# Hybrid encoder layer on one core: the values of the dilated heads are fetched one step earlier, into six buffers instead of four

## The chip, the cores and the metric

The kernel runs on one core of a Trainium2 chip. The core has five engines with a program of their own each: TensorE (PE; its weight loads are shown apart, as PEld), VectorE (DVE), ScalarE (ACT), GpSimd (POOL) and SyncE (SP), which here only issues DMA transfers. Each engine works through its instructions in order and waits on semaphores. The metric is the device time of one execution in microseconds (us), less is better; several runs are summed up by their median. "Granted clock" is the share of its full clock that TensorE was allowed.

## The reference

One encoder layer is applied to a prompt (256 tokens) and to a sample (1024 tokens), model width 1024, all in float32:

```python
h = _rmsnorm(x, g_mix)
z = h @ w_in                       # queries, keys, values of both branches, and the gates
o_a = banded attention, 8 heads, window 128, with a sink
o_b = _dilated_mixture(qb, kb, vb, rel_bias[:, A_HEADS:])
merged = gates[0] * (o_a @ w_branch_a) + gates[1] * (o_b @ w_branch_b)
x = x + merged @ w_out
h = _rmsnorm(x, g_mlp)
x = x + square(relu(h @ w_up)) @ w_down      # then a last _rmsnorm
```

The part that matters is `_dilated_mixture`: three groups of four heads, with (window, dilation) of (128, 1), (512, 4) and (2048, 16). In each group the tokens are sorted by their residue modulo the dilation, every query looks at a band of keys of its own residue, a bias by distance is added, and softmax and the product with the values follow. The three groups' outputs are then mixed by their log-sum-exp.

## The kernel before, in words

The two inputs are treated as 1280 tokens, ten tiles of 128. Products of the layer are split into a high and a low half and done in three matmuls. The work goes in stages: norm and value columns of `w_in`; the other columns of `w_in`, two column blocks at a time ("pairs", function `pair`, line 954), by a seven-product scheme whose matmuls are recorded by one helper (L351, names x, y, z, mm); then the banded attention woven into the last gate columns (L192); the merge and `w_out`; the up and down projections (L351 again). Queries, keys, values and gates pass through DRAM: `scr_qb`, `scr_kb` (queries and keys of the dilated heads, by group), `scr_v` (values), `scr_g` (gates).

The dilated heads are computed by `attention_b`, a generator that is stepped while the last five pairs of columns run. `tick` calls it: at every second call, once all earlier pairs are done, one step of `attention_b` is put between two halves of a product of the pair. The order of every engine's instructions is thus written out by hand; no scheduler moves them.

`attention_b` works on 60 tiles (two pairs of heads, three groups, ten tiles each), two tiles a step. A step of number j (0, 2, 4, ...) issues, in this order:

- `load_v`: the values of two tiles, two or four transfers, from `scr_v` into a buffer named v (L510, queue of SP). A transfer is 128 x 128 float32, 64 KB.
- `values_of`: the product of probabilities and values of tiles j-4 and j-3 on PE (L566, into bank pv), which reads v; then `store_values` copies it out (ACT for one tile, DVE for the other, L271 and L273) and GpSimd's queue writes it to DRAM (L575).
- `transposes` of the probabilities of tiles j-2 and j-1 (PE, L553), copied to SBUF by ACT and DVE.
- `scores` of tiles j and j+1 on PE (L522), then bias and row maximum on DVE (L533, L535).
- `load`: queries and keys of tiles j+4 and j+5 into a buffer named qk (L498, L499, queue of SP; four buffers, so that it has to wait for the scores just issued).
- `exponentials` of tiles j and j+1 on ACT (L543).

SP's queue takes all of these loads in the order of the program, and between them the gate stores (L864, which wait for the tile z that ACT or DVE write) and, at the start of each pair, the two 512 KB blocks of raw weights for the next pair (L381). SP waits at an instruction whose operands are not ready, and everything behind it waits too. Each transfer on this queue also waits for the one issued eight before it: their completions share eight semaphores in turn.

Before the change step j fetches the values of tiles j-2 and j-1, and they are used one step later. Four v buffers hold the tiles of two steps.

After the last pair comes the banded attention's start: its first weights are fetched at L222, its queries, keys and values at L429 to L450, and a part of h returns from DRAM at L622; its first scores are L1071.

Of the kernel before, what the change touches and what calls it, by code (L numbers as in the profile page):

```python
# [15 lines left out]
P = 128  # L16
# [81 lines left out]
def encoder_kernel(  # L98
# [37 lines left out]
    def bank(tag, name=None):  # L136
        return psum.tile([P, 512], F32, name=name or tag, tag=tag, bufs={"mm": 3, "sc": 2, "pt": 2, "pv": 1}[tag])
# [333 lines left out]
    def values_rows(g, i, kt):  # L471

        c = (0, 256, 512 + P)[g] + P * i
        if kt >= 8:
            rows = scr_v[NS:, c : c + P]
            return rows[P * (kt - 8) : P * (kt - 7), :] if g == 0 else rows[kt - 8 :: 2, :]
        rows = scr_v[:NS, c : c + P]
        if g == 0:
            return rows[P * kt : P * kt + P, :]
        return rows[kt // 2 :: 4, :][P * (kt % 2) : P * (kt % 2) + P, :] if g == 1 else rows[kt::8, :]  # L480

    def attention_b(make):
# [4 lines left out]
        n = len(order)  # L487
        held, live, bias = {}, {}, {}
        turned_s = slot("pt", (P, 2, 4, P))

        def load(j):

            if j >= n:
                return
            g, i, t, (pieces, W, _) = order[j]
            qk = held[j] = [make("qk", (P, 3 * P), n=4), None]
            for a, (p0, m, qa, ka) in enumerate(pieces):
                nc.sync.dma_start(qk[0][:, p0 : p0 + m], scr_qb[g][i][:, qa : qa + m])  # L498
                nc.sync.dma_start(qk[0][:, P + P * a : P + P * a + W], scr_kb[g][i][:, ka : ka + W])  # L499
            if t == 0:  # L500
                bias[g, i] = load_bias_b(g, i, make)

        def load_v(j):
            if not 0 <= j < n:
                return
            g, i, t, (pieces, W, _) = order[j]
            v = held[j][1] = make("v", (P, 2, P), n=4)
            for a, (_, _, _, ka) in enumerate(pieces):
                for k in range(W // P):
                    nc.sync.dma_start(v[:, a + k, :], values_rows(g, i, ka // P + k))  # L510

        def scores(j):

            banks = [bank("sc") for _ in range(2)]
            at = lambda k, h: banks[h][:, 2 * P * (k - j) : 2 * P * (k - j) + order[k][3][1]]
            for k in (j, j + 1):
                g, i, t, (pieces, W, c0) = order[k]
                qk = held[k][0]
                for h in range(2):
                    rows = HALVES[h]  # L520
                    for a, (p0, nq, _, _) in enumerate(pieces):
                        nc.tensor.matmul(at(k, h)[p0 : p0 + nq, :], qk[rows, p0 : p0 + nq],  # L522
                                         qk[rows, P + P * a : P + P * a + W], start=True, stop=True,
                                         skip_group_check=True)
            for k in (j, j + 1):
                g, i, t, (pieces, W, c0) = order[k]
                whole, *flat = bias[g, i]
                b = whole[:, :, c0 : c0 + W] if c0 is not None else flat[pieces[0][2] >= NS]
                s = make("s", (P, 2, 2 * P), n=2)
                m = small.tile([P, 2], F32, name="m", tag="m")  # L530
                o = make("o", (P, ROW), n=8)
                for h in range(2):
                    nc.vector.tensor_tensor_reduce(s[:, h, :W], at(k, h), b[:, h, :], 1.0, -3.0e38,  # L533
                                                   op0=ALU.add, op1=ALU.max, accum_out=m[:, h : h + 1])
                nc.vector.tensor_scalar(o[:, 2 * HD : 2 * HD + 2], m, -1.0, None, op0=ALU.mult)  # L535
                live[k] = s, o

        def exponentials(j):
            W = order[j][3][1]
            s, o = live[j]  # L540
            nm, l = o[:, 2 * HD : 2 * HD + 2], o[:, 2 * HD + 2 :]
            for h in range(2):
                nc.scalar.activation(s[:, h, :W], s[:, h, :W], AF.Exp, bias=nm[:, h : h + 1],  # L543
                                     accum_out=l[:, h : h + 1])

        def transposes(j, eng):
            W = order[j][3][1]
            s, o = live[j]
            pt = turned_s[:, j % 2]
            ps = bank("pt")  # L550
            jobs = [(k, h) for k in range(W // P) for h in range(2)]
            for a, (k, h) in enumerate(jobs):
                nc.tensor.transpose(ps[:, P * a : P * a + P], s[:, h, P * k : P * k + P], ident)  # L553
            a = len(jobs)
            moved(eng, pt[:, :a, :], ps[:, : P * a].rearrange("p (i q) -> p i q", q=P))
            live[j] = pt, o

        def values_of(j, whole):

            _, _, _, (pieces, W, _) = order[j]  # L560
            pt, v = live[j][0], held.pop(j)[1]
            pv = whole[:, P * (j % 2) : P * (j % 2) + P]
            for h in range(2):
                for a, (p0, nq, _, _) in enumerate(pieces):
                    for k in range(W // P):
                        nc.tensor.matmul(pv[p0 : p0 + nq, HD * h : HD * h + HD], pt[:, 2 * k + h, p0 : p0 + nq],  # L566
                                         v[:, a + k, HALVES[h]], start=k == 0, stop=k == W // P - 1,
                                         skip_group_check=True)

        def store_values(j, eng, whole):  # L570
            g, i, _, (pieces, _, _) = order[j]
            o = live.pop(j)[1]
            moved(eng, o[:, : 2 * HD], whole[:, P * (j % 2) : P * (j % 2) + P])
            for p0, nq, qa, _ in pieces:
                nc.gpsimd.dma_start(scr_b[g][qa : qa + nq, i, :], o[p0 : p0 + nq, :])  # L575
# [6 lines left out]
        yield  # L582
        yield
        for j in range(0, n + 4, 2):
            load_v(j - 2)
            load_v(j - 1)
            if j > 2:
                pv = bank("pv")
                values_of(j - 4, pv)
                values_of(j - 3, pv)  # L590
                store_values(j - 4, nc.scalar, pv)
                store_values(j - 3, nc.vector, pv)
            if 0 < j <= n:
                transposes(j - 2, nc.scalar)
                transposes(j - 1, nc.vector)
            if j < n:
                scores(j)
            load(j + 4)
            load(j + 5)
            if j < n:  # L600
                exponentials(j)
                exponentials(j + 1)
            yield
# [245 lines left out]
    if True:  # L849
# [179 lines left out]
        for first, last, name in ((0, MIXED, "pairs"), (MIXED, len(PAIRS), "mixed")):  # L1029
            with tc.tile_pool(name=name, bufs=1) as now[0]:  # L1030
                if first:
                    att_b = attention_b(stage)
                for j in range(first, last):
                    if j == len(PAIRS) - 1:
                        hooks = entering()
                    else:
                        hooks = line(j, stage) if j < len(LINES) else iter(())
                    b, p = pair(b, p, PAIRS[j], PAIRS[j + 1] if j + 1 < len(PAIRS) else None, hooks, tick, first)
                run(att_b)
                flush(True)  # L1040
# [160 lines left out]
    if True:  # L1201
# [62 lines left out]
        n = len(order)  # L1264
# [96 lines left out]
        for i, (x, b, c) in enumerate(jobs):  # L1361
            t0, n = BLOCKS[b]
# [179 lines left out]
    class Down:  # L1542
# [4 lines left out]
        def make(self, name, shape=(P, 2, 512), dt=F32):  # L1547
            return self.late.tile(list(shape), dt, name=name, tag="l4", bufs=8)
# [334 lines left out]
```

## Time and profile before

| | |
|---|---|
| median of 3 runs | 1751.15 us (1749.18 to 1754.4) |
| profiled execution, its own time | 1753.6 us |
| its span, first to last instruction | 1751.8 us |
| PE busy | 1713.2 us, 98% of the span |
| DVE, ACT, POOL busy | 976.2, 727.1, 518.8 us |
| mean granted clock of TensorE | 0.996 |
| the stage of the dilated heads | from about 358 to 549 us of the span |

Lines of the profile name the source line, the engine and the tiles written and read: "L566 PE pv<-v,pt" is the values product. "SPq" is the queue of SP, where an instruction issues a transfer; "landing" is the moment when a transfer's completion is seen. A wait is given as who waited, and for whom. In the chain of waits each row is a start, a duration and what the time went to.

### The profile page before, as it was taken

The numbers are of one execution on the slowest core, as the hardware profiler recorded it, in microseconds if no ns is written. First come the engines' busy times: TensorE is split into PE (matmuls) and PEld (weight loads), VectorE is DVE, ScalarE is ACT, GpSimd is POOL, SyncE is SP. The second block draws the span as 40 slices with busy tenths as digits, with TensorE's granted clock in tenths as the row PEclk, the third lists the DMA queues.
The fourth block names the chain that finished last, engine by engine and source line by source line (L and its number), as shares of the span: only waits on it lengthen the run. The fifth ranks groups of instructions, "written<-read, shape, count | busy, mean of one in ns | idle before, by whom it ended". The sixth has DMA issues, their size and how long they took to land.

```text
span 1751.8 us, 25171 instructions
## 1 busy us (share of the span) xinstructions
PE 1713.2 (98%) x9248; PEld 1459.5 (83%) x9248; DVE 976.2 (56%) x1708; ACT 727.1 (42%) x1528; POOL 518.8 (30%) x452
## 2 busy tenths in 40 slices
PE   7999999999999999999999999999999999999998
PEld 6898888878788899978888788888888788888886
DVE  6732323455453466676648645454546876657575
ACT  6232223355553455664336433334334333333344
POOL 0212222212221344300010156454655441305050
PEclk9999999999999999999999999999999999999999
DMA  6414344566555662475212243344336854633333
GB/s 235 143 43 153 98 134 120 144 182 169 162 155 143 211 184 81 124 261 214 94 49 97 84 146 120 118 153 153 117 115 240 299 170 145 221 112 117 114 114 120
DMA packets 214779, 256.35 MB, mean 146 GB/s; under 512 B 24887, under 2 KB 144523, under 8 KB 214528
## 3 DMA queue, kind: packets, MB, share of 16 engines
q1 hardware_dynamic: 201424, 228.26, 40.4%
q0 software_dynamic: 12144, 24.38, 4.6%
q10 hardware_dynamic: 1088, 2.10, 0.3%
q8 instruction: 73, 1.20, 0.3%
q14 instruction: 50, 0.41, 0.1%
HBM read 169.10 MB, written 90.73 MB: 148 GB/s over the span
## 4 chain that ended last, share of the span: by engine, by line
PE 85%; DVE 5%; DMA 4%; ACT 3%; issue 2%; SPq 1%; POOL 1%; DVEq 0%; ACTq 0%; POOLq 0%
PE dn L351 20%; PE x L351 17%; PE mm L192 13%; PE z L351 8%; PE v L739 5%; PE pv L351 5%; PE y L351 4%; PE mm L351 4%; PE pv L1108 2%; PE pv L566 2%; DMA v<-scr_v 1%; PE sc L522 1%; PE pt L1095 1%; PE pt L553 1%; PE tr L342 1%
## 5 line engine op out<-in xcount | busy, mean ns | idle before, releaser
L351 PE MATMUL dn<-dhi,ulo 128*128 128x512 f32 x448 | 174.6, 390 | 2.6 <-DVE ulo L186 2.6
L351 PE MATMUL dn<-dhi,uhi 128*128 128x512 f32 x448 | 174.3, 389 | 0.0
L351 PE MATMUL dn<-dlo,uhi 128*128 128x512 f32 x448 | 174.3, 389 | 0.0
L351 PE MATMUL x<-chi,wlo 128*128 128x512 f32 x424 | 167.8, 396 | 2.0 <-DVE u L1756 1.4
L351 PE MATMUL x<-clo,whi 128*128 128x512 f32 x424 | 165.9, 391 | 0.1
L351 PE MATMUL x<-chi,whi 128*128 128x512 f32 x424 | 165.1, 389 | 0.0
L318 DVE TENSOR_TENSOR wlo<-ta,whi 128x1024 fp32r<-128x1024 f32 x30 | 55.8, 1858 | 181.7 <-ACT whi L316 181.7
L318 DVE TENSOR_TENSOR wlo<-raw,whi 128x1024 fp32r<-128x1024 f32 x60 | 89.1, 1484 | 101.9 <-ACT whi L316 101.9
L393 POOL TENSOR_TENSOR tb<-raw 128x512 f32<-128x512 f32 x25 | 33.3, 1333 | 361.5 <-PE mm L192 137.7
L351 PEld LDWEIGHTS dn<-dhi,ulo 128*128 128x128 f32 x448 | 84.1, 188 | 21.0 <-DVE ulo L186 3.6
L186 DVE TENSOR_TENSOR ulo<-uraw,uhi 128x1024 fp32r<-128x1024 f32 x56 | 95.0, 1717 | 11.7 <-ACT uhi L185 11.7
L351 PEld LDWEIGHTS dn<-dlo,uhi 128*128 128x128 f32 x448 | 84.1, 188 | 17.4
L351 PEld LDWEIGHTS dn<-dhi,uhi 128*128 128x128 f32 x448 | 84.1, 188 | 17.4
L351 PEld LDWEIGHTS x<-chi,wlo 128*128 128x128 f32 x424 | 79.9, 188 | 20.7 <-issue 3.4
L351 PEld LDWEIGHTS x<-chi,whi 128*128 128x128 f32 x424 | 79.7, 188 | 17.1
L351 PEld LDWEIGHTS x<-clo,whi 128*128 128x128 f32 x424 | 79.9, 189 | 14.8 <-DVE clo L318 0.4
L1581 POOL TENSOR_TENSOR t<-raw,t 128x1024 f32<-128x1024 f32 x16 | 46.8, 2940 | 141.8 <-DMA raw<-in_w_down_dram 141.8
L1732 DVE TENSOR_TENSOR v<-v,dn 128x512 f32<-128x512 f32 x90 | 59.5, 682 | 43.1 <-PE dn L351 38.5
L1828 POOL TENSOR_TENSOR u<-u,u 128x640 f32<-128x640 f32 x16 | 25.6, 1597 | 164.4 <-ACT u L1753 164.4
L351 PE MATMUL pv<-phi,wlo 128*128 128x256 f32 x256 | 72.5, 283 | 1.7 <-ACT u L1752 1.7
L543 ACT ACTIVATE s<-s,o 128x128 f32<-128x128 f32 (+1 forms) x120 | 51.9, 434 | 52.3 <-DVE o L535 48.3
L351 PE MATMUL dn<-dhi,up 128*128 128x512 f32 x224 | 73.5, 389 | 0.0
(337 smaller groups left out, 4784.8 us busy)
## 6 DMA issues: line engine op xcount, KB each, us to landing
scr_u<-u SPq DMA_DIRECT2D x112, 320.0 KB, 2.6
uraw<-scr_u SPq DMA_DIRECT2D x56, 512.0 KB, 4.2
raw<-in_w_in_dram SPq DMA_DIRECT2D x33, 512.0 KB, 5.5
raw<-in_w_up_dram SPq DMA_DIRECT2D x32, 512.0 KB, 5.5
raw<-in_w_down_dram SPq DMA_DIRECT2D x28, 512.0 KB, 6.2
sg<-scr_g SPq DMA_DIRECT2D x32, 256.0 KB, 5.4
uraw<-scr_u SPq DMA_DIRECT2D x28, 256.0 KB, 4.2
v<-scr_v SPq DMA_DIRECT2D x96, 64.0 KB, 2.3
```

The source lines that it names most:

```text
L186: nc.vector.tensor_tensor(lo, src, hi.bitcast(F32), op=ALU.subtract)
L192: nc.tensor.matmul(ps, a, b, start=i == 0, stop=i == len(seq) - 1)
L318: nc.vector.tensor_tensor(lo, src, hi.bitcast(F32), op=ALU.subtract)
L351: nc.tensor.matmul(ps, a, b, start=first and i == 0, stop=last and i == len(seq) - 1, skip_group_check=True)
L393: (nc.vector if vector else nc.gpsimd).tensor_tensor(o, x, y, op=ALU.subtract)
L543: nc.scalar.activation(s[:, h, :W], s[:, h, :W], AF.Exp, bias=nm[:, h : h + 1], accum_out=l[:, h : h + 1])
L566: nc.tensor.matmul(pv[p0 : p0 + nq, HD * h : HD * h + HD], pt[:, 2 * k + h, p0 : p0 + nq], v[:, a + k, HALVES[h]], start=k == 0, stop=k == ...
L739: nc.tensor.matmul(ps[:, :n], a, b, start=k == 0 and j == 0, stop=k == KC - 1 and j == 2)
L1108: nc.tensor.matmul(pv[:, HD * h : HD * h + HD], pt[:, 2 * b + h, :], src, start=b == 0, stop=b == W // P - 1)
L1581: nc.gpsimd.tensor_tensor(o, a, b, op=ALU.subtract)
L1732: nc.vector.tensor_tensor(v, v, ps, op=ALU.add)
L1828: nc.gpsimd.tensor_tensor(u[S1], u21, u22, op=ALU.add)
```

## The change

Step j now fetches the values of tiles j and j+1, whose scores are computed in the same step, instead of those of tiles j-2 and j-1. They are used two steps later instead of one. The tiles of three steps are then held at once, so v has six buffers instead of four; a buffer is 1 KB in each partition. The first step, which fetched no values, now fetches those of the first two tiles; the fetches end one step earlier than before. The program issues the same 96 transfers. On PE, DVE, ACT and GpSimd the order of the work stays as it was; on SP the fetches stand in the same places with other tiles.

```diff
@@ def load_v(j):
             g, i, t, (pieces, W, _) = order[j]
-            v = held[j][1] = make("v", (P, 2, P), n=4)
+            v = held[j][1] = make("v", (P, 2, P), n=6)
             for a, (_, _, _, ka) in enumerate(pieces):
                 for k in range(W // P):
                     nc.sync.dma_start(v[:, a + k, :], values_rows(g, i, ka // P + k))
@@ the loop of attention_b
         for j in range(0, n + 4, 2):
-            load_v(j - 2)
-            load_v(j - 1)
+            load_v(j)
+            load_v(j + 1)
             if j > 2:
                 pv = bank("pv")
                 values_of(j - 4, pv)
```

## The prediction

> **What bounds the kernel now.** I read the page first, then busy time by stage, then the waits, the chain and the timelines of the one stage that the change touches.
>
> ```profile
> PE 1713.2 (98%) x9248; PEld 1459.5 (83%) x9248; DVE 976.2 (56%) x1708; ACT 727.1 (42%) x1528; POOL 518.8 (30%) x452
> ```
>
> TensorE (PE) is busy 98% of the span: only a pause of PE, or a slower clock, can be won back. The busy time of two stretches (start:end, length, busy of PE, PEld, DVE, ACT, POOL, then the granted clock, the DMA share and GB/s):
>
> ```profile
> 358.00:549.00 191.00, 182.34 (x1294) 149.00 (x1293) 95.39 (x398) 99.50 (x334) 43.78 (x79) 0.97 0.57 162
> 549.00:575.00 26.00, 26.00 (x143) 22.65 (x143) 8.47 (x10) 6.95 (x10) 6.45 (x12) 1.00 0.65 182
> ```
>
> The first is the dilated attention, woven into the column pairs; the second is the rest of those pairs. PE idles 191.00 - 182.34 = 8.66 us in the first, at a mean clock of 0.97, and not at all in the second. The waits of this stretch (who waited, for whom, us in all, times, longest):
>
> ```profile
> PE pv L566 <- DMA v<-scr_v: 8.3, 6, 3.5
> PEld pv L566 <- ACT s L543: 1.3, 3, 0.6
> PEld pv L566 <- DMA v<-scr_v: 0.9, 1, 0.9
> PE pv L566 <- ACT z L936: 0.2, 1, 0.2
> ```
>
> So nearly all idle time of PE in this stage stands before the values matmul (L566) and ends when a tile of v lands. PE's timeline gives the places (start, length, idle before in brackets):
>
> ```profile
> 367.83 1.08 PE L566 MATMUL pv<-v,pt 128*128 128x64 f32 x8 [1.41 <-DMA v<-scr_v]
> 475.39 1.94 PE L566 MATMUL pv<-v,pt 128*128 128x64 f32 x8 [3.53 <-DMA v<-scr_v]
> 533.53 2.10 PE L566 MATMUL pv<-v,pt 128*128 128x64 f32 x16 [1.71 <-DMA v<-scr_v]
> ```
>
> The other three are 1.6 us together (8.3 less 1.41, 3.53 and 1.71). Why v is late stands in the rows of SP's queue, which issues every load here in order:
>
> ```profile
> 361.11 1.01 SPq L381 DMA_DIRECT2D raw<-in_w_in_dram  x2
> 362.17 1.85 SPq L510 DMA_DIRECT2D v<-scr_v  x2
> ...
> 435.13 0.32 SPq L864 DMA_DIRECT2D scr_g<-z  x1
> ...
> 474.77 0.32 SPq L499 DMA_DIRECT2D qk<-scr_kb  x1
> ...
> 527.85 5.48 SPq L510 DMA_DIRECT2D v<-scr_v  x8
> ```
>
> Two causes. At 361, and in the same way ahead of the v loads at 468.9 and 527.85, the two 512 KB weight loads of the next pair are issued just before v, and v lands late behind them: at 468.9 the chain shows 6.39 us from issue to landing, where the median of L510 is 2.3 (a row below). At 435.13 it is SP that is late: a gate store (L864), which waits for its z, stands ahead of v.
>
> ```profile
> 468.87 6.39 DMA v<-scr_v
> 475.39 1.94 PE pv L566 x8
> 477.33 0.85 PE pt L553 x4
> 478.18 1.79 PE sc L522 x12
> 479.97 1.90 PE x L351 x6
> 483.26 0.84 PE pv L566 x8
> 484.10 0.66 PE pt L553 x6
> 484.76 1.01 PE sc L522 x12
> 485.77 1.60 PE z L351 x6
> ...
> 535.63 1.28 PE pt L553 x6
> 536.91 1.79 PE sc L522 x12
> ```
>
> The chain also shows a second loss: after the two longest pauses the same work takes longer. The granted clock says why (third number from the end; 0.50 is half):
>
> ```profile
> 470.40:473.80 3.40, 1.46 (x7) 0.85 (x5) 0.00 (x0) 1.54 (x7) 0.00 (x0) 1.00 1.07 312
> 473.80:480.60 6.80, 5.21 (x26) 3.83 (x27) 1.28 (x5) 0.66 (x2) 1.07 (x2) 0.50 0.38 109
> 531.80:535.20 3.40, 1.69 (x16) 1.70 (x16) 0.00 (x0) 0.53 (x2) 0.00 (x0) 1.00 0.66 183
> 535.20:538.60 3.40, 3.40 (x21) 2.12 (x20) 0.72 (x2) 0.87 (x2) 1.07 (x2) 0.50 0.12 40
> ```
>
> **The change part by part.** *The load moves one step up.* In step j SP now issues v of tiles j and j+1 where it issued j-2 and j-1. Count (96 issues), bytes, place in SP's queue and engine stay; only which tile is fetched differs. A v that PE missed by up to 3.5 us is now wanted one step later. A step lasts about 5 us or more (at full clock 0.84+0.44+1.01 and two halves of a product group such as the 1.60, about 5). The two worst: v that landed at 475.3 (468.87 + 6.39) would be wanted one step after 471.7 (475.39 less the pause and its ramp), about 476.8, so 1.5 us to spare; v that landed at 533.4 is wanted a step after 531.7, about 537, so 3.5 us to spare. At 362 the first load moves ahead of the weights altogether. So I take all these waits as gone: 8.3 + 0.9 = **9.2 us**.
>
> *The three short waits named "ACT s" and the one named "ACT z" (1.5 us).* They stand before the same matmul, and exp (ACT s, L543) is not among its operands; SP's timeline has the v loads of these three steps 2.3 to 3.7 us ahead, about a median landing. If all are v's: 1.5; if none: 0. I take the middle, **0.7**.
>
> *The half clock.* First place: 1.94+0.85+1.79+1.90 = 6.48 against 0.84+0.44+1.01+1.60 = 3.89 at full clock (0.44 is two thirds of the 0.66, four transposes for six), 2.6 us. Second: 1.28+1.79 = 3.07 against 0.66+1.01 = 1.67, 1.4 us. Bound from the clock rows: 5.21 and 3.40 us of busy PE at half speed can give back half, 4.3; from below, 2.6 if the second spell had no cost. I take **4.0 us**, the sum of the rows.
>
> The Trainium skill, page "TensorE: Matmul & The Clock Gate", section "HAM oscillation", says that gaps over about 3.4 us are what lets the clock drop. By that rule the 1.71 us pause would have cost no clock, the sum would be 1.4 less and the time 1740. The trace disagrees: 0.50 at 535.20:538.60 after a window with half of it idle (1.69 of 3.40 busy).
>
> *Cost: waits of PE.* With more outstanding v loads, PE's instruction list grows by 9 separate waits.
>
> ```profile
> L566 PEldq EVENT_SEMAPHORE  x60: 51/51/276, 367.7 to 545.5; - x60
> ```
>
> (Duration in ns, least, median, most.) The landing of the v loads (L510), then of the qk loads:
>
> ```profile
> DMA to landing us min/median/max: 1.7/2.3/6.4
> ```
>
> ```profile
> DMA to landing us min/median/max: 1.7/2.2/4.3
> ```
>
> At 51 ns these are 0.46 us when nothing hides them, 0 when the running matmul does: **0.4**. *Cost: queues.* The first v pair stands one step earlier, ahead of the qk loads of tiles 4 and 5: two issues of 0.43 us, covered because SP has to wait there for the first scores before it may load tile 4; that cover gone, 0.9 us on loads wanted two steps later: 0. POOL's queue is not passed. The buffer that a v load takes was last read by the values matmul of tile j-6, one step ago, as before: no new stop of SP. The qk loads (landing in 2.2 us) are wanted two steps after issue; losing the pauses brings their use up to 6.1 us nearer (3.5+2.6 at 475); the tightest, the last of which is issued at 474.77, are used by the scores at 484.76, then at 478.7: 3.9 us after issue, 1.7 to spare at the median.
>
> *What is late next.* The transposes (L553) wait for exp on ACT:
>
> ```profile
> 471.29 0.18 ACT L543 ACTIVATION_READ_ACCUMULATOR s<-s,o 128x1 f32 x1
> ```
>
> The exp of the step that paused longest ended at 471.5, and the transposes would now start at 471.7 + 0.84 = 472.5: 1 us to spare, with PE the only bound of the stage.
>
> Sum: 9.2 + 0.7 + 4.0 - 0.4 = **13.5 us**. The profiled execution took 1753.6 (its span 1751.8 and 1.8 around it), which gives 1740.1. The profiled time is 2.45 above the median of the runs, 1751.15; those runs (1749.18 to 1754.4) may have lost less in these waits. From the median it would be 1737.7. As what remains is the same in both, I take **1739**, nearer the profiled one.
>
> **The rivals.**
> (a) *qk takes over.* SP issues qk behind v; with PE not pausing, qk's 1.7 us of slack at 475 and the like at 533 may fail, as landings reach 4.3. Then PE waits at the scores (L522) instead: back come 2 us of pause and 2 of half clock there, and perhaps 1 at 533: gain 8.5, **1745**. For it: a DMA share of 0.57 on average, with the weights in it. Against: no wait of L522 for a DMA stands in the list now. It decides if a qk landing takes over 3.9 us there.
> (b) *Given back at the next stage.* Its start hangs on transfers:
>
> ```profile
> 572.50 7.04 DMA hhi<-scr_h
> ```
>
> If those ended at a fixed time, most of the gain would go: 1753.6 - 3 = **1750**. Against: each is issued after a store or a buffer that PE itself releases (hhi at 572.50, right as PE ends), so they move with PE.
> (c) *Slower.* The first weight fetch for the next stage
>
> ```profile
> 558.72 0.39 SPq L222 DMA_DIRECT2D raw<-in_w_in_dram  x1
> ```
>
> now carries a wait for PE in the program, which an earlier wait of SP used to cover. If that wait stands for the pair's last matmuls, this fetch and all loads of the next stage behind it go from 558.72 to 572.5: up to 13.8 us of PE idle, and two spells of half clock of 3.4 us, 1.7 each: 1740.1 + 13.8 + 3.4 = **1757**. It decides once the hold gives back more than the 13.5 won. Against: the old wait that covered it was for values matmuls at 533, long done.
> (d) *The change does nothing:* excluded as far as order goes, since v's issues do stand one step earlier.
>
> **How the numbers follow.** Forecast 0.78, (a) 0.10, (b) 0.07, (c) 0.05. A measurement of this kernel cannot tell under 0.3% (5.3 us) from no change: below 1745.9 is faster. The forecast and most of (a) count as faster: 0.87; (b) and a rest as same: 0.08; (c) as slower: 0.05. The forecast's own bounds: 9.2 + 4.3 + 1.5 off the median give 1736; 9.2 + 2.6 - 0.5 off the profiled time give 1742. Runs differ by 2 to 3 us to either side of their median, which takes the low end to 1733; the high end goes to (a), 1746.
>
> **What would show it.** Right: in the stage from 358, now about 177 us long, no PE wait for v at L566, PE idle under 1 us, clock 1.00 throughout, and everything after 549 the same but some 13 us earlier. Wrong: waits at L522 for qk (a); a longer stretch between the last pair and the first scores at L1071 (b, c); half clock left in the stage.

## The result and the profile after

| | before | after |
|---|---|---|
| median of 4 runs | 1751.81 us (1749.18 to 1754.4) | 1736.28 us (1735.58 to 1737.51) |
| profiled execution, its own time | 1753.6 us | 1735.73 us |
| its span | 1751.8 us | 1734.0 us |
| mean granted clock of TensorE | 0.996 | 0.999 |

Before has one run more here than at the prediction (1752.47 us), which moves its median from 1751.15 us. The ratio of the times is 0.9912, with a 95% interval of 0.9895 to 0.9929: the change makes the kernel 15.5 us faster by the medians, 17.9 us by the two profiled executions. The first line of the page of the kernel after, and the line of its part 1:

```profile
span 1734.0 us, 25189 instructions
...
PE 1705.5 (98%) x9248; PEld 1455.9 (84%) x9248; DVE 976.3 (56%) x1708; ACT 727.0 (42%) x1528; POOL 520.7 (30%) x452
```

PE's busy time went from 1713.2 to 1705.5 us with the same 9248 matmuls. 7.7 us of the gain is thus time in which PE is drawn as busy, the rest is idle time that is gone. The stage, by windows of the kernel after (columns as in the prediction):

```profile
358.00:532.00 174.00, 174.00 (x1287) 144.90 (x1286) 94.00 (x396) 98.31 (x334) 43.03 (x77) 1.00 0.63 175
532.00:558.00 26.00, 26.00 (x140) 22.51 (x139) 9.30 (x12) 6.95 (x10) 7.20 (x12) 1.00 0.68 187
```

PE is busy through the whole of the stage at a clock of 1.00; before it was busy 182.34 of 191.00 us at 0.97. The list of waits of the kernel after, in the stage, holds no row in which PE itself waits for a transfer. Of the rows of its weight loads (PEld, which run beside a matmul) these are the largest and the one that names v:

```profile
PEld sc L522 <- issue: 5.7, 24, 0.4
...
PEld sc L522 <- DMA v<-scr_v: 1.0, 3, 0.3
```

The first stood in the list of before as well, with 7.2 us. Neither stops PE, since the windows row shows PE busy for 174.00 of 174.00 us.

Where the gain stands can be read from the starts of the same instructions. First those of before on PE's timeline: the first scores of the stage, its last values matmul, and the first scores of the banded attention behind it.

```profile
358.74 0.71 PE L522 MATMUL sc<-qk 64*128 64x128 f32 x8
...
546.24 1.38 PE L566 MATMUL pv<-v,pt 128*128 128x64 f32 x16
...
578.60 0.28 PE L1071 MATMUL sc<-kk,q 128*128 128x256 f32 x1
```

The same three of the kernel after:

```profile
357.71 0.71 PE L522 MATMUL sc<-qk 64*128 64x128 f32 x8
...
530.08 1.38 PE L566 MATMUL pv<-v,pt 128*128 128x64 f32 x16
...
562.43 0.28 PE L1071 MATMUL sc<-kk,q 128*128 128x256 f32 x1
```

The differences are 1.03, 16.16 and 16.17 us. So 15.1 us were won inside the stage, and none was lost or won between it and the first scores behind it. 1.03 us had already been won ahead of the stage, in work that the change doesn't touch: from 14.36 to 16.41 us of the span the matmuls of before (L739) still start every 0.43 us, as at half clock, and those of the kernel after every 0.23 us. The other 1.7 of the 17.9 us come later: 1.2 from a pause of PE ahead of the transposes of the banded attention (L1095), some 0.4 from shorter pauses behind it. That first pause was 1.27 us in before and 0.04 in the kernel after; over all executions profiled here it was anything from 0 to 1.27 us, with and without the change, so it is not put down to the change.

### The profile page after: what moved, and what is told of

The parts are those of the page before. It is cut to its first block, busy times and chain, and to the rows that moved or that the text cites. A ratio compares the mean times of both kernels' runs of the same rounds, so it can differ in the third digit from the quotient of the medians.

```text
span 1734.0 us, 25189 instructions
## 1 busy us (share of the span) xinstructions
PE 1705.5 (98%) x9248; PEld 1455.9 (84%) x9248; DVE 976.3 (56%) x1708; ACT 727.0 (42%) x1528; POOL 520.7 (30%) x452
## 4 chain that ended last, share of the span: by engine, by line
PE 89%; DVE 4%; ACT 2%; DMA 2%; issue 2%; POOL 1%; SPq 0%; DVEq 0%; ACTq 0%; POOLq 0%
PE dn L351 21%; PE x L351 17%; PE mm L192 13%; PE z L351 9%; PE v L739 5%; PE pv L351 5%; PE mm L351 5%; PE y L351 4%; PE pv L1108 2%; PE pv L566 2%; PE sc L522 2%; PE pt L553 1%; PE pt L1095 1%; PE tr L342 1%; PE sc L1071 1%
```

## The experiments

The first four kernels ran on one chip, where the kernel before had a median of 1754.4 us (1750.62 to 1762.64); the other four on a second chip, where it had 1754.26 us (1751.97 to 1760.48). Each ratio is to the runs of before on the same chip. The theory: v came late because one step of lead was too short for a fetch that stands behind late or large transfers in SP's queue, and a second step of lead covers that. The rivals: it is the number of buffers that matters; it is something else that the change moves; the clock, not the pauses, is what was won.

**Six buffers without the earlier fetch.**

```diff
-            v = held[j][1] = make("v", (P, 2, P), n=4)
+            v = held[j][1] = make("v", (P, 2, P), n=6)
```

> Only the buffers of v are six; the fetch stays one step ahead of its use. If the lead is what counts: no change, 1751.8 within 2 us, with the waits for v at the values matmul as before (about 8 to 10 us of PE idle). Rival, that the number of buffers or their place in memory did it: most of the gain, about 1738.

Measured: 1753.65 us (1751.75 to 1756.4), ratio 0.999 (0.9976 to 1.0004). The waits that the change removes are all there, in this kernel's list of waits, and on PE's timeline at the known places:

```profile
PE pv L566 <- DMA v<-scr_v: 9.0, 6, 3.2
```

```profile
474.69 1.08 PE L566 MATMUL pv<-v,pt 128*128 128x64 f32 x8 [3.21 <-DMA v<-scr_v]
...
532.71 2.02 PE L566 MATMUL pv<-v,pt 128*128 128x64 f32 x14 [2.52 <-DMA v<-scr_v]
```

More buffers alone do nothing. In the list of SP's own waits of before, too, the v loads wait for transfers alone (2.4 us in all), never for the values matmul that would free a buffer.

**The earlier fetch without more buffers.** The fetch of tiles j and j+1 goes behind the values matmuls and the stores of the same step, so that four buffers are enough; the lead is two steps less the length of that piece.

```diff
         for j in range(0, n + 4, 2):
-            load_v(j - 2)
-            load_v(j - 1)
             if j > 2:
                 ...
                 store_values(j - 3, nc.vector, pv)
+            load_v(j)
+            load_v(j + 1)
```

> Four buffers, and the fetch of tiles j and j+1 stands right behind the values matmuls of tiles j-4 and j-3 in the same step, so that it can take the buffers that these just read. If the lead is what counts: nearly two steps of it remain (less the 1 to 2 us of the values matmul that SP now has to wait for), so no wait for v over 0.5 us and 1736 to 1738. Rival, that SP stopping there makes the queries and keys late: waits at the scores and about 1745.

Measured: 1736.45 us (1735.52 to 1740.32), ratio 0.9898 (0.9876 to 0.9919), the same as the change. The stage by its windows:

```profile
349.00:533.00 184.00, 184.00 (x1341) 153.44 (x1340) 98.56 (x401) 103.18 (x340) 44.82 (x80) 1.00 0.63 177
```

No pause is left. By the starts on PE's timeline the stage takes 172.37 us from the first scores to the last values matmul (358.31 to 530.68), as long to the hundredth as in the kernel after (357.71 to 530.08); in before it is 187.50. The lead is the whole of the change; the two buffers are only what the place of the fetch in the step asks for.

**Three steps ahead.** Six buffers, tiles j+2 and j+3 at the place of the kernel above.

```diff
-            v = held[j][1] = make("v", (P, 2, P), n=4)
+            v = held[j][1] = make("v", (P, 2, P), n=6)
...
         load(3)
+        load_v(0)
+        load_v(1)
...
-            load_v(j - 2)
-            load_v(j - 1)
             if j > 2:
                 ...
+            load_v(j + 2)
+            load_v(j + 3)
```

> Six buffers and a fetch nearly three steps ahead (of tiles j+2 and j+3, behind the values matmuls). If two steps already hide every landing (least slack 1.25 us in the changed kernel): 1736, within 1.5 us of the changed kernel. Rival, that v still holds back something that the wait list does not show: 1733 or less.

Measured: 1736.95 us (1736.22 to 1737.15), ratio 0.9894 (0.9872 to 0.9916). PE is as full as with two steps, and the time is the same:

```profile
349.00:533.00 184.00, 184.00 (x1342) 153.40 (x1341) 98.37 (x401) 103.38 (x340) 44.63 (x80) 1.00 0.63 177
```

The stage takes 172.37 us here too (358.50 to 530.87). A third step of lead has nothing left to hide.

**No step ahead.** Four buffers, each fetch in the step of its use.

```diff
-            load_v(j - 2)
-            load_v(j - 1)
+            load_v(j - 4)
+            load_v(j - 3)
```

> The fetch in the step of its own use, four buffers. If the lead is what counts: the load is issued about when PE wants it, so each of the 30 steps waits a landing of 2.4 to 3 us, 75 to 90 us in all, four of them 4 us more behind the weights, and the pauses pull the clock down for part of the stage, 20 to 40 us more: about 1860, between 1830 and 1890. Rival, that the waits for v come only from the weights and the gate stores ahead of it in the queue: about 1765.

Measured: 1889.77 us in one run, at the upper end of what was expected. The list of waits of its stage, then the stage by its windows:

```profile
PE pv L566 <- DMA v<-scr_v: 87.5, 29, 5.8
```

```profile
358.00:686.00 328.00, 240.11 (x1294) 189.43 (x1293) 98.18 (x398) 100.71 (x335) 44.02 (x80) 0.79 0.34 95
```

PE stands idle 87.9 us (328.00 less 240.11), and the same 1294 matmuls that took 182.34 us in before take 240.11 at a mean clock of 0.79. Of the 137 us that this stage is longer, 79 are idle time and 58 are clock. Zero, one, two and three steps of lead thus give 1890, 1754, 1736 and 1737 us.

**The weights behind v.** The kernel before, with its one step of lead, but each pair's two 512 KB weight loads (L381) are issued behind the v loads of the next step instead of in front of them.

```diff
+    pending = []
...
             load_v(j - 1)
+            while pending:
+                next(pending.pop(), None)
...
             if late:
-                next(nb, None)
+                pending.append(nb)
...
                 next(att_b, None)
+                while pending:
+                    next(pending.pop(), None)
```

> The kernel before (four buffers, one step ahead), with the next pair's two weight loads issued behind the v loads of the next step instead of ahead of them. If the place of the weights in the queue is the first cause: the three pauses at 367, 475 and 533 and both spells of half clock go, 1.6 + 6.1 + 3.5 = 11 us, about 1741; the pauses at 408 and 440 and the short ones stay, some 3 us of PE idle. Rival, that v is late there because the transfers share the engines whatever their order: under 4 us of gain, 1748 or more.

Measured: 1745.26 us (1741.07 to 1746.86), ratio 0.9946 (0.9931 to 0.9961): 9.0 us by the medians, where I had expected 11, and the rival allowed for under 4. The profiled execution was the fastest of them by 3.4 us, 1741.07 us, so its trace may show less of what is left than the others would. In its list of waits (the values matmul is L568 here, two lines further down) this is left:

```profile
PEld pv L568 <- ACT s L545: 3.0, 5, 1.3
PE pv L568 <- DMA v<-scr_v: 2.2, 5, 0.9
```

The pauses at 367 and 533 are gone, that at 475 is down from 3.53 to 0.94 us, and the clock stays at 1.00 through the stage. I had expected the pauses at 408 and 440 to stay; that at 440 did (0.74 us at 436.32), but of the 1.2 us at 408 only 0.16 are left.

**The gate stores off SP's queue.** The kernel before, with the gate stores (L864) of this stage issued on GpSimd's queue.

```diff
             while stores and (all_ or stores[0][0] + 1 < ticks[0]):
-                nc.sync.dma_start(*stores.pop(0)[1:])
+                (nc.gpsimd if ticks[0] > 18 * MIXED else nc.sync).dma_start(*stores.pop(0)[1:])
```

> The kernel before, with the gate stores of this stage issued on GpSimd's queue instead of SP's. If SP's stop at those stores is the second cause: the pauses at 408 and 440 and the three short ones go, about 3 us, 1748.5; the long ones behind the weights stay. Rival, that GpSimd's queue frees the gate tiles late and PE waits for a bank instead: slower, 1755 or more.

Measured: 1747.36 us (1745.81 to 1750.54), ratio 0.996 (0.9945 to 0.9974): 6.9 us, more than twice what I expected. PE's timeline shows the pauses that are left:

```profile
366.84 1.08 PE L566 MATMUL pv<-v,pt 128*128 128x64 f32 x8 [1.20 <-DMA v<-scr_v]
...
417.46 1.08 PE L566 MATMUL pv<-v,pt 128*128 128x64 f32 x8 [1.33 <-DMA v<-scr_v]
...
472.12 1.19 PE L566 MATMUL pv<-v,pt 128*128 128x64 f32 x5 [3.15 <-DMA v<-scr_v]
...
529.30 0.96 PE L566 MATMUL pv<-v,pt 128*128 128x64 f32 x7 [0.45 <-ACT s L543]
```

The small pauses at 408 and 440, which stood behind late gate stores, are gone. The one at 533, which I had put down to the weights, went from 1.71 to 0.45 us, and it is gone too where the weights stand behind v: taking away either cause does away with most of it. It seems to have needed both, the weights ahead of v and an SP that came late to them: SP issues these weights at 522.00 here and at 526.75 in before, 6.9 and 5.1 us ahead of the moment when PE begins to wait. At 417, behind the weights issued at 409.09, a new pause of 1.33 us has appeared.

**Both causes away.** The edits of the last two kernels together, with four buffers and one step of lead.

> The kernel before with both edits: weights behind v, gate stores on GpSimd's queue; still four buffers and one step ahead. If these two causes are all: 14 to 15 us, 1737 to 1738, as fast as the changed kernel, with no wait for v over 0.3 us. Rival, that one step is too short whatever the queue holds: 2 us or more of waits for v left, 1740 or more.

Measured: 1738.46 us (1736.94 to 1739.02), ratio 0.9909 (0.9894 to 0.9923): 15.8 us, where the two edits alone gave 9.0 and 6.9, and where the change gives 0.9912. One pause is left on PE's timeline:

```profile
472.89 1.08 PE L568 MATMUL pv<-v,pt 128*128 128x64 f32 x8 [0.76 <-DMA v<-scr_v]
```

So these two causes are what made v late. One step of lead is just about enough for a queue in which v stands behind neither; the change leaves the queue as it is and lets the lead cover it.

**Pauses of chosen lengths.** To see when the clock drops, sixteen pauses of PE are put into the pairs of the kernel before: a transpose that waits for a chain of DVE operations of varying length. It leaves no computation out and adds only these.

```diff
+        def pause(ps):
+            nap = stage("nap", (P, 256))
+            nc.vector.tensor_copy(nap, ps[:, :256])
+            for _ in range(next(naps)):
+                nc.vector.tensor_tensor(nap, nap, nap, op=ALU.max)
+            nc.tensor.transpose(bank("pt", "nap")[:, :P], nap[:, :P], ident)
...
```

> The kernel before with 16 pauses of PE put into the pairs ahead of the dilated heads (a copy on DVE, then 0 to 12 steps of a 128x256 maximum, then a transpose on PE that needs them): roughly 0.7 to 5 us each, 35 to 45 us in all. If the clock drops after a 3.41 us window that is about half idle: pauses under 1.7 us never cost clock, those over 3.4 nearly always, those between by their place in the window. Rival, that only a gap over 3.4 us does it: no half clock after any pause of 1.8 to 3.3 us.

Measured: 1849.49 us in one run; the pauses came out longer than planned, 1.55 to 6.70 us. Three of them on PE's timeline:

```profile
225.67 0.47 PE L961 MATMUL nap<-ident,nap 128*128 128x128 f32 x1 [2.45 <-DVE nap L960]
...
264.14 0.34 PE L961 MATMUL nap<-ident,nap 128*128 128x128 f32 x1 [2.55 <-DVE nap L960]
...
302.19 0.33 PE L961 MATMUL nap<-ident,nap 128*128 128x128 f32 x1 [3.01 <-DVE nap L960]
```

And the granted clock around them (third number from the end), in stretches of 3.41 us that begin where the clock's own changes in this trace put them:

```profile
221.99:225.40 3.41, 1.23 (x6) 0.69 (x4) 3.16 (x5) 1.10 (x2) 0.00 (x0) 1.00 0.46 134
225.40:228.82 3.42, 3.15 (x15) 3.15 (x16) 1.35 (x2) 0.00 (x0) 0.00 (x0) 0.50 0.35 102
259.54:262.95 3.41, 2.05 (x10) 1.36 (x8) 2.37 (x4) 1.93 (x3) 0.00 (x0) 1.00 0.51 153
262.95:266.36 3.41, 2.22 (x19) 2.22 (x20) 2.20 (x4) 0.00 (x0) 0.00 (x0) 1.00 0.54 151
266.36:269.78 3.42, 3.42 (x21) 2.97 (x20) 0.00 (x0) 0.39 (x1) 1.29 (x1) 1.00 0.00 0
297.08:300.50 3.42, 2.10 (x10) 1.40 (x8) 2.33 (x4) 1.97 (x3) 0.00 (x0) 1.00 0.52 155
300.50:303.91 3.41, 1.72 (x15) 1.73 (x16) 2.66 (x5) 0.00 (x0) 0.00 (x0) 1.00 0.52 152
303.91:307.32 3.41, 3.41 (x23) 3.04 (x22) 0.00 (x0) 0.39 (x1) 1.29 (x1) 1.00 0.00 0
```

A pause of 2.45 us, 2.18 of it in one stretch, halves the clock for the next stretch. Longer pauses of 2.55 and 3.01 us, which lie across the border of two stretches with at most 1.69 us in either, cost no clock. So it isn't the length of a pause that decides but how much of one such stretch is idle. Of the sixteen pauses the one under 1.7 us cost no clock and all eleven over 3.4 us did; of the four between, that of 2.45 us did and those of 1.99, 2.55 and 3.01 us did not. The rival, that only a gap over 3.4 us does it, is refuted by the pause of 2.45 us.

## Why the prediction was right

The predicted time was 1739 us (1733 to 1746) and the median is 1736.28: the forecast case came about, faster by more than it said. By its steps:

- **The waits for v are gone** (9.2 us, and 0.7 for the short ones): right, and under-sized. By the starts of PE's instructions, the pauses and the short waits cost some 11.2 us: 1.6 at 367, 1.5 at 408, 0.7 at 440, 3.7 at 475, 2.1 at 533, and 1.6 at four places (383, 389, 462, 518) where before shows a weight load that waits or a pause of 0.2 us. I had summed the idle time of the list of waits, and a pause costs more than that. The matmuls of the kernel after, before and at the values of the step where before paused longest:

```profile
470.34 0.39 PE L351 MATMUL z<-hlo,whi 128*128 128x512 f32 x1
470.57 0.39 PE L351 MATMUL z<-hhi,whi 128*128 128x512 f32 x1
470.80 1.00 PE L566 MATMUL pv<-v,pt 128*128 128x64 f32 x8
```

  They start every 0.23 us and are drawn 0.39 us long. When nothing follows, the idle time is counted from that drawn end, 0.16 us after the next one would have started. By the starts, 0.16 us are missing at five of the seven idle times on PE, 0.07 and 0.12 at the other two: 1.0 of the missing 1.3 us. The short waits named after ACT, of which I took half, were v's altogether: they are gone when v comes earlier, and there was no other edit.
- **The half clock** (4.0 us): right. The two spells cost 2.4 and 1.4 us by the starts, 3.8 together, and none is left in the stage.
- **More waits of PE** (0.4 us): the cost was not there, though the waits came, and at another line than the one I had shown. L566 has 60 of them before and after. It is the scores (L522) that have 20 more, first before, then after:

```profile
L522 PEldq EVENT_SEMAPHORE  x78: 51/51/51, 355.8 to 534.7; - x78
```

```profile
L522 PEldq EVENT_SEMAPHORE  x98: 51/51/51, 354.8 to 520.0; - x98
```

  Those of L566 in the kernel after:

```profile
L566 PEldq EVENT_SEMAPHORE  x60: 51/51/1416, 361.8 to 528.0; - x60
```

  One of them lasts 1.42 us, where the longest in before was 0.28. The trace puts its end down to the copy of pv by DVE (L273), not to a transfer. PE is busy without a break while all of them pass, so none costs time.

- **The sum**: 13.5 us forecast for the stage, 15.1 measured (11.2 and 3.8, with rounding). The step that was mis-sized is the first, by 1.3 us, and the 0.4 of cost did not come. From the median of before this gives 1751.81 - 15.1 = 1736.7, and 1736.28 was measured. Of the 2.7 us between the forecast and the median, 1.6 us are thus the two terms; the rest comes from the time that I subtracted them from, which I had chosen nearer the profiled execution than the median. How much an execution at the median loses in the stage no trace shows, so it is in part luck that 1736.7 and 1736.28 agree so closely.
- **Which causes made v late** (weights ahead of it, and SP late at the gate stores): shown by the three kernels that take away one, the other and both. That I gave the pause at 533 to the weights alone was wrong, by the kernel with the stores on another queue.
- **The slack**: I gave v at 475 1.5 us. In the kernel after, SP's timeline has v behind the same weights here:

```profile
461.57 1.44 SPq L381 DMA_DIRECT2D raw<-in_w_in_dram  x2
463.06 3.57 SPq L510 DMA_DIRECT2D v<-scr_v  x2
```

  The first of these two v loads, issued at 463.06, landed at 469.54, and the row of 470.80 above uses it: 1.25 us to spare, the least in the stage. At 533, where I had given 3.5, it is 3.4 (landing at 521.96, use at 525.32). A landing of 6.5 us that would have stopped PE in before lies inside the second step of lead. The longest landing of a v load in this kernel is 8.0 us, issued at 408.82 behind the weights of 407.66; its values matmul starts at 420.05, so 3.1 us were to spare there.
- **Rival (a), qk takes over**: did not happen, and came nearer than I said. The landing times of the queries (L498) in the kernel after:

```profile
DMA to landing us min/median/max: 1.8/2.3/5.8
```

  The longest is 5.8 us (5.5 for the keys, L499), where before had at most 4.3, perhaps because PE no longer pauses while the weights pass. The tile that these belong to still had 4.7 us to spare. The loads that I had called the tightest landed at 471.50, 0.88 us ahead of the first scores of their step (472.39), where I had 1.7; the matmul that reads them starts at 473.02, 1.52 us later than the landing. Some 1.5 us more there would, as far as this goes, have brought a wait at L522; with three steps of lead the same load had 0.4 us to spare, and PE still did not wait.
- **Rival (b), given back at the next stage**: did not happen. The first scores of the banded attention moved by 16.17 us, as much as the stage's last values matmul.
- **Rival (c), the first weight fetch held by PE**: did not happen. The fetch on SP's timeline of the kernel after:

```profile
542.56 0.38 SPq L222 DMA_DIRECT2D raw<-in_w_in_dram  x1
```

  It stands 12.48 us behind the last values matmul (530.08), exactly as in before (558.72 and 546.24). Its wait for PE held up nothing.
- **The clock rule**: against the rule of the Trainium skill, page "TensorE: Matmul & The Clock Gate", section "HAM oscillation", I had taken the 1.71 us pause as one that costs clock. The half clock behind that pause stands in the trace of before. The kernel with chosen pauses adds that 2.45 us is enough, and that 2.55 and 3.01 us need not be; the next section gives what the traces have in common.

## What to carry to other kernels

- Where small fetches share an in-order queue with large or late ones, count their lead in steps of the consumer against the longest landing behind those, not against the median: here 2.3 us is the median, and the longest was 6.4 us in before and 8.0 in the kernel after, with a step of about 5 us. Beyond that a longer lead is worth nothing (1736 and 1737 us for two and three steps), short of it each step is worth much (1890, 1754).
- Moving a fetch inside its step can give nearly the same lead with fewer buffers: 1736.45 us with four, 1736.28 with six.
- A short pause of a TensorE that is otherwise full costs its idle time, a little that the trace draws as busy, and sometimes most of it again in clock (here 3.53 us of idle time cost 3.7 and 2.4 us, 1.71 cost 2.1 and 1.4); so count the pauses that fill near half of a clock stretch, not only the long ones.

## What the runs showed of the hardware that I had not expected

- **When the clock halves.** The granted clock of every trace changes only on a grid of 3.41 us, and a half-clock spell lasts 3.41 or 6.83 us (10.24 in three of the twenty-odd spells with no step of lead). Laid over PE's records of all profiled executions, no grid stretch at full clock that was idle for less than 41% (1.39 us) is followed by half clock, and each one idle for more than 57% (1.95 us) is. Between these both occur: before's 1.71 us at 533 halved it, and this stretch of before, with 1.67 us idle, did not:

```profile
1361.26:1364.67 3.41, 1.74 (x8) 1.17 (x7) 3.41 (x2) 1.29 (x2) 3.41 (x2) 1.00 0.53 172
```

  The Trainium skill, page "TensorE: Matmul & The Clock Gate", section "HAM oscillation", states that gaps over about 3.4 us are what costs the clock. The traces differ: a pause of 1.7 us can be enough, and one of 3.01 us need not be. What decides inside the band, and what sets the length of a spell, stays open.
- **The causes of the late v add up, as far as the noise lets one see.** Taking the weights out from before v gave 9.0 us, taking the gate stores off SP 6.9, both 15.8; each is known to some 2.5 us. In the one profiled execution of each, the stage from the first scores to the last values matmul is 10.8, 5.0 and 14.1 us shorter than in before, together less than the sum, as it has to be where a pause like that at 533 goes with either cause. I had expected much less of the stores, since only two short pauses stood directly behind them. I take it that a late SP also issues the weights and the v behind them late, so that one cause lengthens the pauses of the other; the pause at 533 is the one place where the traces show it.
- **Pauses make the time vary.** The 17 runs of before spread over 12 us on one chip (1750.62 to 1762.64), the six of the kernel with three steps of lead over 1 us (1736.22 to 1737.15), the six with two steps in four buffers over 5 us. I take it that where the pauses fall on the clock's grid differs from run to run. Only one execution of each kernel has a trace, so this is argued; but the mean granted clock is on record for each run, and in before it is 0.997 in the three fastest of the 17 and 0.993 to 0.995 in the five longest.
